# First mixer of a two-layer encoder: items in pairs, float32r masks, and value products placed behind the transposes of the weights

## The chip, the cores and the metric

The kernel runs on one core of one Trainium2 chip. The metric is the device time of one execution in microseconds (us). The core's engines are called as the profile calls them: PE is the matrix engine (PEld its weight loads), DVE the vector engine, ACT the scalar engine with the activation functions, POOL the general engine, SP the one that issues most transfers.

## The reference

A trunk of two layers is applied to two sequences, a prompt of 256 rows and a sample of 512 rows, 1024 wide, all in float32. Each layer runs a token mixer and then a SwiGLU block, each between two RMS norms, with a residual sum. The mixer of layer 0, the one that the change touches, is a windowed attention: 16 query heads of 64 in 4 groups, each group with one key and one value head, and a learned logit per head (a sink) in the denominator. A query row sees the keys at a distance of at most 128.

```
sc = einsum('bqkgd,bskd->bkgqs', qi, kb)
valid = (abs(qpos - kpos) <= WINDOW) & (kpos >= 0) & (kpos < s)
sc = where(valid, sc, -inf)
m = maximum(max(sc), sink)
e = exp(sc - m)
p = e / (sum(e) + exp(sink - m))
o = einsum('bkgqs,bskd->bqkgd', p, vb)
```

The mixer of layer 1 is a differential attention without a window; the change leaves it alone.

## The kernel before

The 768 rows are six tiles of 128 (tiles 0 and 1 the prompt, 2 to 5 the sample). Weight products run in float32r, with each operand split into a high and a low part, so that each 128-deep step of a product is three matrix products (L315, L316, L317). ACT makes the high part, DVE the low part.

The first mixer (`mixer_a`) goes through 24 units: for each of the 4 key heads, the six row tiles. `unit(i)` projects 384 columns (four query heads, one key and one value head) in eight steps and one end step, which applies the rotary positions and splits. Two units later a `turn` transposes the split queries and keys on PE (L609, L611) and ACT copies them out.

Attention follows its unit by `LAG` = 4 units. It is cut into 96 items (unit i, query head j of the four). `score` makes the scores of one item: queries times the high part of the keys (L630), times their low part (L631), and then, where a neighbouring key tile is only half inside the window, a product of an identity with a mask (L633 for the left, L635 for the right neighbour), which adds -3e38 to what must not be seen. Identity and masks are bf16 and 128 columns wide. Units with two key tiles (row tiles 0, 1, 2, 5) have one mask, those with three (row tiles 3, 4) have two. DVE takes the maximum (L637) and its negative with the sink (L640), ACT the exponential with its sum (L646) and that of the sink (L648). `normalize` makes the denominator on DVE (L655, L656) and scales the weights (L657). `turn_e` transposes the weights on PE, one product of 128 columns in full fp32 for each key tile (L666), and ACT copies them to a buffer of the unit (L670), heads 0 and 2 in one half of it, heads 1 and 3 in the other. `values` multiplies them with the values in full fp32 (L680): for each key tile one product for heads 0 and 2 and one for heads 1 and 3, which take the two halves of 64 output rows; the profile counts two instructions for each.

The order is written out in the loop at L704. `item(n)` issues the score of item n, the normalization of n-1 and the transposes of n-3. For each unit the list `att` holds four such items and then the value products of the unit before; `weave` spreads these five entries evenly among the nine or ten steps of the projection. From unit 23 on a special order holds, in which the output projection takes the place of the projection. The framework that builds the program keeps each engine's list in the order of the source, except that it moves later work in front of an instruction whose operands, by its own reckoning, are not ready.

The weights `e` of two items share one of three 128x1024 buffers (tag `y` of the pool `scr`), which also hold the normalized input tiles at the start. All products write to eight PSUM banks.

Of the kernel before, what the change touches and what calls it, by code (L numbers as in the profile page):

```python
# [8 lines left out]

F32 = mybir.dt.float32  # L10
F32R = mybir.dt.float32r
BF16 = mybir.dt.bfloat16
AF = mybir.ActivationFunctionType
ALU = mybir.AluOpType
AX = mybir.AxisListType
# [2 lines left out]
P = 128  # L18
D = 1024
# [19 lines left out]
def seq_of(t):  # L39
    for first, n in SEQS:  # L40
        if first <= t < first + n:
            return first, n
    raise ValueError(t)
# [3 lines left out]
def trunk(  # L47
# [19 lines left out]
    nc = tc.nc  # L67
    const = ctx.enter_context(tc.tile_pool(name="const", bufs=1))
# [5 lines left out]
    scr = ctx.enter_context(tc.tile_pool(name="scr", bufs=3))  # L74
# [3 lines left out]
    def bank(name):  # L78
        return ps.tile([P, 512], F32, tag="ps", name=name)


    ident = const.tile([P, P], F32, name="ident")
    make_identity(nc, ident)
    ident_r = const.tile([P, P], F32R, name="ident_r")
    nc.vector.tensor_copy(out=ident_r, in_=ident)
    ident_b = const.tile([P, P], BF16, name="ident_b")
    nc.vector.tensor_copy(out=ident_b, in_=ident)

    masks = []
    for name, step, mult in (("mask_l", 1, -1), ("mask_r", -1, 1)):  # L90
        m = const.tile([P, P], BF16, name=name)
        nc.gpsimd.memset(m, 0.0)
        nc.gpsimd.affine_select(
            out=m, in_=m, compare_op=ALU.is_ge, fill=MASK, base=0,
            pattern=[[step, P]], channel_multiplier=mult,
        )
        masks.append(m)
    cos_sb = const.tile([P, 4, HD], F32, name="cos_sb")
    sin_sb = const.tile([P, 4, HD], F32, name="sin_sb")
    mhalf = const.tile([P, 8], F32, name="mhalf")  # L100
# [190 lines left out]
    def take(n):  # L291

        i = state["used"]
        state["used"] += n
        prepare(i + n)
        return [parts.pop(j) for j in range(i, i + n)]
# [74 lines left out]
    def new_y(name):  # L371
        return scr.tile([P, D], F32, tag="y", name=f"y_{name}")
# [165 lines left out]
    def column_blocks(taken, width):  # L538
        return [tuple(w[:, j * width:(j + 1) * width] for w in s) for s in taken for j in range(2)]

    def out_unit(t, wk, o, n2, gp, sq, name):

        pm = bank(name)
        steps = product_steps(pm, [(htile(t, k), wk[k]) for k in range(KT)])
        if t == NT - 1:
            steps = releasing(steps, 4)
        return steps + [lambda: project_end(t, pm, o, n2, gp, sq, name)]  # L550
# [16 lines left out]
    def mixer_a(gp, g_next, first_steps, o):  # L567
        with ExitStack() as st:
# [53 lines left out]
            def score(i, j):  # L622
                gi, t = divmod(i, NT)
                first, n = seq_of(t)
                k0, k1 = max(first, t - 1), min(first + n, t + 2)
                nk = k1 - k0
                keys = slice((k0 - first) * P, (k1 - first) * P)
                s = bank(f"sc{i}_{j}")[:, :nk * P]
                left, right = k0 < t, k1 > t + 1
                nc.tensor.matmul(s, q[i][:, j], kh[gi, first][:, keys], start=True, stop=False)  # L630
                nc.tensor.matmul(s, q[i][:, j], kl[gi, first][:, keys], start=False, stop=not (left or right))  # L631
                if left:
                    nc.tensor.matmul(s[:, :P], ident_b, masks[0], start=False, stop=not right)  # L633
                if right:
                    nc.tensor.matmul(s[:, (nk - 1) * P:], ident_b, masks[1], start=False, stop=True)  # L635
                mx = small.tile([P, 1], F32, tag="mx", name=f"mx{i}_{j}")
                nc.vector.tensor_reduce(out=mx, in_=s, axis=AX.X, op=ALU.max)  # L637
                h = gi * 4 + j
                negm = small.tile([P, 1], F32, tag="negm", name=f"negm{i}_{j}")
                nc.vector.tensor_scalar(  # L640
                    out=negm, in0=mx, scalar1=-HD ** -0.5, scalar2=nsink[:, h:h + 1], op0=ALU.mult, op1=ALU.min)
                if j % 2 == 0:
                    e2[0] = new_y(f"e{i}_{j}")
                e = e2[0][:, j % 2 * 512:j % 2 * 512 + nk * P]
                den = small.tile([P, 2], F32, tag="den", name=f"den{i}_{j}")
                nc.scalar.activation(  # L646
                    out=e, in_=s, func=AF.Exp, bias=negm, scale=HD ** -0.5, accum_out=den[:, 0:1])
                nc.scalar.activation(out=den[:, 1:2], in_=negm, func=AF.Exp, bias=sink[:, h:h + 1])  # L648
                blocks[i, j] = e, den
# [3 lines left out]
            def normalize(i, j):  # L653
                e, den = blocks[i, j]
                nc.vector.tensor_tensor(out=den[:, 0:1], in0=den[:, 0:1], in1=den[:, 1:2], op=ALU.add)  # L655
                nc.vector.reciprocal(out=den[:, 0:1], in_=den[:, 0:1])  # L656
                nc.vector.tensor_scalar(out=e, in0=e, scalar1=den[:, 0:1], scalar2=None, op0=ALU.mult)  # L657
# [3 lines left out]
            def turn_e(i, j):  # L661
                e, _ = blocks.pop((i, j))
                nk = e.shape[1] // P
                tp = bank(f"tpe{i}_{j}")
                for c in range(nk):
                    nc.tensor.transpose(tp[:, c * P:(c + 1) * P], e[:, c * P:(c + 1) * P], ident)  # L666
                if j == 0:

                    eTs[i] = ap.tile([P, 3, 2, 2, P], F32, tag="eT", name=f"eT{i}", bufs=2)
                nc.scalar.copy(  # L670
                    out=eTs[i][:, :nk, j % 2, j // 2], in_=tp[:, :nk * P].rearrange("p (c n) -> p c n", c=nk))

            def values(i):
                gi, t = divmod(i, NT)
                first, n = seq_of(t)
                k0, k1 = max(first, t - 1), min(first + n, t + 2)
                po, eT = bank(f"poa{i}"), eTs.pop(i)
                for c in range(k1 - k0):
                    for r in range(2):
                        nc.tensor.matmul(  # L680
                            po[r * HD:(r + 1) * HD, :256], vv[gi, first][:, k0 + c - first],
                            eT[:, c, r].rearrange("p h n -> p (h n)"), start=(c == 0), stop=(c == k1 - k0 - 1))
                nc.scalar.copy(out=o[t][:, gi * 256:(gi + 1) * 256], in_=po[:, :256])

            def split_o(t):
                half, at = t // 3, (t % 3) * P
                split(h_hi[half][:, :, at:at + P], h_lo[half][:, :, at:at + P],
                      o[t].rearrange("p (k n) -> p k n", k=KT))

            LAG = 4  # L690
            n_units = 4 * NT
            items = [(i, j) for i in range(n_units) for j in range(4)]
            n_items = len(items)

            def item(n):
                if n < n_items:
                    score(*items[n])
                if 1 <= n <= n_items:
                    normalize(*items[n - 1])
                if 3 <= n <= n_items + 2:  # L700
                    turn_e(*items[n - 3])

            wk_o, sq = [], {}
            for i in range(n_units + LAG):  # L704
                if i < n_units:
                    fill = unit(i)
                    at = 4 if i == 0 else 3
                    fill = fill[:at] + first_steps.pop(i, []) + fill[at:]
                else:
                    t = i - n_units  # L710
                    if t == 0:
                        wk_o = column_blocks(take(4), 512)
                    fill = out_unit(t, wk_o, o, 0, gp, sq, f"po0_0_{t}")
                if i - 2 in pending:
                    fill = fill[:4] + [pending.pop(i - 2)] + fill[4:]
                att = []
                if i >= LAG:
                    for j in range(4):
                        n = (i - LAG) * 4 + j
                        att.append(lambda n=n: item(n))  # L720
                    if i > LAG:
                        att.append(lambda i=i: values(i - LAG - 1))
                if i >= n_units - 1:

                    t = i - n_units + 1
                    fill = (att[:1] + fill[:2] + att[1:2] + fill[2:3] + att[2:3] + fill[3:4] + att[4:] + fill[4:5]
                            + [lambda t=t: split_o(t)] + att[3:4] + fill[5:])
                    att = []
                weave(att, fill)

            fill = out_unit(LAG, wk_o, o, 0, gp, sq, f"po0_0_{LAG}")
            att = [lambda n=n: item(n) for n in range(n_items, n_items + 4)] + [lambda: values(n_units - 1)]
# [746 lines left out]
```

## Time and profile before

| | |
|---|---|
| time, median of 3 runs (lowest to highest) | 1687.2 us (1686.35 to 1689.65) |
| the profiled execution | 1688.34 us |
| its span from first to last instruction | 1686.6 us |
| mean granted clock of PE | 0.997 |
| PE busy in the span | 98% |
| DVE busy in the span | 74% |
| ACT busy in the span | 56% |

The profiled execution is one run with the profiler on; all times of instructions are read from it, in us from the start of its span. A group such as `sc<-mask_l,ident_b` names what is written, what streams through PE and what is loaded as weights. The length of a matrix product in the profile contains its way through the array and overlaps with the next one, so that what a product costs in a row of products is the distance to the start of the next.

### The profile page before, as it was taken

The page shows a single profiled execution, that of the slowest core. Times are in us where ns is not written, and L with a number is a line of the kernel's source. Part 1 is how long each engine was busy: PE and PEld are TensorE (multiplying, and loading weights), DVE is VectorE, ACT ScalarE, POOL GpSimd, SP SyncE. Part 2 cuts the span into 40 slices and gives each one's busy share as a digit, 9 for nine tenths or more (in the row PEclk, how much of TensorE's full clock was granted, in tenths as well). Part 3 has the DMA queues.
Part 4 walks back from the last instruction along what each step waited for, and adds up shares of the span by engine and source line. Part 5 has one row for each costly group of instructions (what it writes and reads, how often), then busy time and mean ns, then how long its engine had stood idle before and what let it go on. Part 6 is the DMA issues. An engine that isn't in the chain of part 4 may idle for free. (4 is left out here: it accounts for less than half of the span.)

```text
span 1686.6 us, 25513 instructions
## 1 busy us (share of the span) xinstructions
PE 1659.1 (98%) x9483; PEld 1514.3 (90%) x9483; DVE 1251.3 (74%) x2488; ACT 949.7 (56%) x2158; POOL 81.7 (5%) x104
## 2 busy tenths in 40 slices
PE   7999999999999999999999999999899999999998
PEld 7888878899999998888999999988799999998887
DVE  7888766896766666988777676874997666666886
ACT  6777775654444444556566666674744444444553
POOL 1000001000000000001000000331000000000001
PEclk9999999999999999999999999999999999999999
DMA  6111014534333347666211111113444343336765
GB/s 212 39 38 48 14 38 150 175 134 140 109 125 99 128 139 250 230 235 205 83 39 38 38 38 38 48 51 113 170 138 141 108 141 108 128 114 226 249 222 176
DMA packets 62107, 207.30 MB, mean 123 GB/s; under 512 B 6752, under 2 KB 8928, under 8 KB 61728
## 3 DMA queue, kind: packets, MB, share of 16 engines
q1 hardware_dynamic: 55152, 175.15, 30.8%
q0 software_dynamic: 6688, 30.28, 5.6%
q8 instruction: 74, 1.21, 0.3%
q14 instruction: 49, 0.40, 0.1%
q10 hardware_dynamic: 144, 0.26, 0.0%
HBM read 162.80 MB, written 42.86 MB: 122 GB/s over the span
## 5 line engine op out<-in xcount | busy, mean ns | idle before, releaser
L223 DVE TENSOR_TENSOR wlo<-wraw,whi 128x1024 fp32r<-128x1024 f32 (+2 forms) x180 | 204.9, 1144 | 173.9 <-ACT whi L222 172.7
L222 ACT CAST whi<-wraw 128x1024 fp32r<-128x1024 f32 (+2 forms) x180 | 176.5, 986 | 117.4 <-PE py L316 58.9
L315 PE MATMUL py<-hhi,whi 128*128 128x384 f32 x464 | 155.4, 335 | 0.8 <-ACT u L976 0.8
L317 PE MATMUL py<-hhi,wlo 128*128 128x384 f32 x464 | 155.0, 334 | 0.0
L316 PE MATMUL py<-hlo,whi 128*128 128x384 f32 x464 | 155.0, 334 | 0.0
L315 PE MATMUL pqb<-whi,hhi 128*128 128x384 f32 x384 | 136.5, 356 | 0.0
L316 PE MATMUL pqb<-wlo,hhi 128*128 128x384 f32 x384 | 128.9, 336 | 0.0
L317 PE MATMUL pqb<-whi,hlo 128*128 128x384 f32 x384 | 128.8, 335 | 0.0
L303 ACT CAST hhi<-araw 128x768 fp32r<-128x768 f32 (+1 forms) x74 | 57.6, 783 | 94.6 <-DMA araw<-act 94.2
L317 PE MATMUL pv<-whi,hlo 128*128 128x512 f32 (+1 forms) x240 | 92.2, 384 | 0.4 <-DVE hlo L304 0.4
L315 PE MATMUL pv<-whi,hhi 128*128 128x512 f32 (+1 forms) x240 | 92.4, 385 | 0.0
L316 PE MATMUL pv<-wlo,hhi 128*128 128x512 f32 (+1 forms) x240 | 92.1, 384 | 0.0
L304 DVE TENSOR_TENSOR hlo<-araw,hhi 128x768 fp32r<-128x768 f32 (+1 forms) x74 | 65.2, 889 | 32.3 <-ACT hhi L303 32.1
L315 PEld LDWEIGHTS py<-hhi,whi 128*128 128x128 f32 x464 | 87.1, 188 | 1.7 <-ACT u L976 1.4
L316 PEld LDWEIGHTS py<-hlo,whi 128*128 128x128 f32 x464 | 87.1, 188 | 0.0
L317 PEld LDWEIGHTS py<-hhi,wlo 128*128 128x128 f32 x464 | 87.1, 188 | 0.0
L315 PE MATMUL po<-whi,hhi 128*128 128x512 f32 x192 | 77.9, 406 | 0.2 <-ACT hhi L303 0.2
L317 PE MATMUL po<-whi,hlo 128*128 128x512 f32 x192 | 75.4, 393 | 0.2 <-DVE hlo L304 0.2
L316 PE MATMUL po<-wlo,hhi 128*128 128x512 f32 x192 | 75.3, 392 | 0.0
L315 PEld LDWEIGHTS pqb<-whi,hhi 128*128 128x128 f32 x384 | 72.3, 188 | 2.0 <-issue 1.7
L315 PE MATMUL pqa<-whi,hhi 128*128 128x384 f32 x192 | 73.9, 385 | 0.0
L315 PE MATMUL px<-hhi,whi 128*128 128x384 f32 x208 | 70.8, 342 | 2.7 <-ACT hhi L303 2.7
(303 smaller groups left out, 4829.6 us busy)
## 6 DMA issues: line engine op xcount, KB each, us to landing
act<-st POOLq DMA_DIRECT2D x22, 1344.0 KB, 6.6
wraw<-in_wgu SPq DMA_DIRECT2D x56, 512.0 KB, 4.6
araw<-act SPq DMA_DIRECT2D x70, 384.0 KB, 4.0
y_wraw<-in_wgu SPq DMA_DIRECT2D x40, 512.0 KB, 3.6
wraw<-in_wd SPq DMA_DIRECT2D x40, 512.0 KB, 3.9
wraw<-in_wb SPq DMA_DIRECT2D x32, 384.0 KB, 3.2
xd<-x SPq DMA_DIRECT2D x18, 512.0 KB, 3.0
x<-xd SPq DMA_DIRECT2D x18, 512.0 KB, 4.1
```

The costliest lines, as they stand in the source:

```text
L222: state["raw_hi"] = nc.scalar.copy(out=hi, in_=src)
L223: state["raw_lo"] = nc.vector.tensor_tensor(out=lo, in0=src, in1=hi.bitcast(F32), op=ALU.subtract)
L303: state["hi"] = nc.scalar.copy(out=hi, in_=src)
L304: state["lo"] = nc.vector.tensor_tensor(out=lo, in0=src, in1=hi.bitcast(F32), op=ALU.subtract)
L315: nc.tensor.matmul(out, ah, bh, start=start and i == 0, stop=False, skip_group_check=more)
L316: nc.tensor.matmul(out, ah, bl, start=False, stop=False, skip_group_check=more)
L317: nc.tensor.matmul(out, al, bh, start=False, stop=stop and i == last, skip_group_check=more)
```

## The change

Three things are changed. The identity for the masks and the masks themselves become float32r: the masks are built as f32 by POOL in a scratch tile and cast by DVE. `item` can issue two scores one after the other; then it normalizes all items before n and transposes all up to n-3. Units 4 to 22 of the loop (attention of units 0 to 18) use it with two items at a time, so that `att` has two entries instead of four; the rest goes one by one as before. And in these units the value products are no entry of their own but are issued right behind the second pair, whose transposes are the last two heads of the same unit.

```
-    ident_b = const.tile([P, P], BF16, name="ident_b")
-    nc.vector.tensor_copy(out=ident_b, in_=ident)
     masks = []
+    row = scr.tile([P, D], F32, tag="y", name="mask_rows")
     for name, step, mult in (("mask_l", 1, -1), ("mask_r", -1, 1)):
-        m = const.tile([P, P], BF16, name=name)
+        m = row[:, len(masks) * P:(len(masks) + 1) * P]
         nc.gpsimd.memset(m, 0.0)
         nc.gpsimd.affine_select(
             out=m, in_=m, compare_op=ALU.is_ge, fill=MASK, base=0,
             pattern=[[step, P]], channel_multiplier=mult,
         )
-        masks.append(m)
+        masks.append(const.tile([P, P], F32R, name=name))
+        nc.vector.tensor_copy(out=masks[-1], in_=m)
...
-                    nc.tensor.matmul(s[:, :P], ident_b, masks[0], start=False, stop=not right)
+                    nc.tensor.matmul(s[:, :P], ident_r, masks[0], start=False, stop=not right)
...
-                    nc.tensor.matmul(s[:, (nk - 1) * P:], ident_b, masks[1], start=False, stop=True)
+                    nc.tensor.matmul(s[:, (nk - 1) * P:], ident_r, masks[1], start=False, stop=True)
...
-            def item(n):
-                if n < n_items:
-                    score(*items[n])
-                if 1 <= n <= n_items:
-                    normalize(*items[n - 1])
-                if 3 <= n <= n_items + 2:
-                    turn_e(*items[n - 3])
+            done = {"normed": 0, "turned": 0}
+
+            def item(n, several=1):
+
+                for m in range(n, min(n + several, n_items)):
+                    score(*items[m])
+                while done["normed"] < min(n, n_items):
+                    normalize(*items[done["normed"]])
+                    done["normed"] += 1
+                while done["turned"] < min(n - 2, n_items):
+                    turn_e(*items[done["turned"]])
+                    done["turned"] += 1
...
                 if i >= LAG:
-                    for j in range(4):
+
+                    step = 2 if i < n_units - 1 else 1
+                    for j in range(0, 4, step):
                         n = (i - LAG) * 4 + j
-                        att.append(lambda n=n: item(n))
+                        att.append(lambda n=n, step=step: item(n, step))
                     if i > LAG:
-                        att.append(lambda i=i: values(i - LAG - 1))
+                        value = lambda i=i: values(i - LAG - 1)
+                        if step == 1:
+                            att.append(value)
+                        else:
+                            att[-1:] = [lambda a=att[-1], value=value: (a(), value())]
```

More of the change, by code (lines that the diff above doesn't have):

```diff
@@ L11 @@
 F32R = mybir.dt.float32r
-BF16 = mybir.dt.bfloat16
 AF = mybir.ActivationFunctionType
```

## The prediction

> **What bounds the kernel now.** I read the page first, then the busy time of the first mixer's stretch, then the matrix engine's timeline inside it. The page's first line:
>
> ```profile
> span 1686.6 us, 25513 instructions
> ```
>
> The change touches only the first mixer's attention and the constants ahead of it. Its stretch, in the view of busy time by window (window, length, then PE, PEld, DVE, ACT, POOL):
>
> ```profile
> 34.00:256.00 222.00, 221.56 (x1513) 185.43 (x1512) 174.19 (x636) 166.41 (x573) 0.00 (x0) 1.00 0.12 37
> ```
>
> PE is busy 221.56 of 222.00 us and the clock is full; DVE with 174.19 and ACT with 166.41 have room, which covers two scores' reductions and exponentials arriving at once (if it doesn't, the last rival holds). So what counts is how long PE takes for its own list, and whether the new order makes it wait. A busy PE says nothing about gaps between products (ends are modelled), so I take distances from one start to the next. The timeline of PE (start, length, line, operation, count):
>
> ```profile
> 151.67 0.23 PE L633 MATMUL sc<-mask_l,ident_b 128*128 128x128 bf16 x1
> 151.71 0.42 PE L315 MATMUL pqa<-whi,hhi 128*128 128x384 f32 x1
> 152.00 0.41 PE L666 MATMUL tpe<-ident,y_e 128*128 128x128 f32 x2
> 152.17 0.42 PE L316 MATMUL pqa<-wlo,hhi 128*128 128x384 f32 x1
> 152.43 0.34 PE L317 MATMUL pqa<-whi,hlo 128*128 128x384 f32 x1
> ...
> 152.95 0.34 PE L317 MATMUL pqa<-whi,hlo 128*128 128x384 f32 x1
> 153.22 1.08 PE L680 MATMUL poa<-eT,va 128*64 128x256 f32 x8
> 154.24 0.44 PE L315 MATMUL pqa<-whi,hhi 128*128 128x384 f32 x1
> 154.52 0.34 PE L316 MATMUL pqa<-wlo,hhi 128*128 128x384 f32 x1
> ...
> 155.10 0.23 PE L635 MATMUL sc<-mask_r,ident_b 128*128 128x128 bf16 x1
> 155.17 0.39 PE L666 MATMUL tpe<-ident,y_e 128*128 128x128 f32 x2
> 155.32 0.42 PE L315 MATMUL pqa<-whi,hhi 128*128 128x384 f32 x1
> 155.58 0.33 PE L316 MATMUL pqa<-wlo,hhi 128*128 128x384 f32 x1
> 155.75 0.34 PE L317 MATMUL pqa<-whi,hlo 128*128 128x384 f32 x1
> ```
>
> Three things are to be seen. A projection product of 384 columns takes 0.17 (155.58 to 155.75). A bf16 mask followed by transposes takes 0.07 (155.10 to 155.17). And the order on the chip is not the source's: at 151.71 one projection product stands between a mask and the transposes that the source puts directly behind it, so work that is not yet ready is passed by later work that is.
>
> **The change part by part.** Of the 24 units (4 key heads by 6 row tiles), 0 to 18 go in pairs: 76 items, 38 pairs. Units with two key tiles have one mask per item (13 units, 26 pairs), units with three have two (6 units, 12 pairs). Units 19 to 23 keep single items: 12 with one mask, 8 with two. The value products directly behind transposes are those of units 0 to 17, 18 calls. Instruction counts of DVE and ACT stay, except in the constants.
>
> First, transposes in one group instead of two. Two transposes and the projection product behind them run from 155.17 to 155.58; less that product's 0.17 they cost 0.24. For three key tiles:
>
> ```profile
> 174.20 0.23 PE L633 MATMUL sc<-mask_l,ident_b 128*128 128x128 bf16 x1
> 174.27 0.22 PE L635 MATMUL sc<-mask_r,ident_b 128*128 128x128 bf16 x1
> 174.32 0.50 PE L666 MATMUL tpe<-ident,y_e 128*128 128x128 f32 x3
> 174.57 0.43 PE L315 MATMUL pqa<-whi,hhi 128*128 128x384 f32 x1
> ```
>
> Three stand 0.25 ahead of the next product against 0.15 for two: 0.10 to 0.11 for each further one. A group of four is then 0.24 + 0.21 = 0.45 against 2 x 0.24 = 0.48, a gain of 0.03 a pair: 38 x 0.03 = -1.1 us. Switching from transposes to products costs very little here, which is the first reason why I expect no large gain.
>
> Second, the masks in float32r. The weight loads of PE:
>
> ```profile
> 155.10 0.10 PEld L635 LDWEIGHTS <-ident_b 128*128 128x128 bf16 x1
> 155.12 0.21 PEld L666 LDWEIGHTS tpe<-ident,y_e 128*128 128x128 f32 x2
> 155.29 0.19 PEld L315 LDWEIGHTS pqa<-whi,hhi 128*128 128x128 f32 x1
> 155.40 0.19 PEld L316 LDWEIGHTS pqa<-wlo,hhi 128*128 128x128 f32 x1
> ```
>
> The load of a float32r operand lasts 0.19, that of the bf16 identity 0.10. Where no long product covers them, two float32r loads start 0.11 apart (155.29, 155.40). A float32r mask streams only 128 columns, so the load for what follows is not covered: I take 0.11 where another mask or a score follows. Where transposes follow, I keep 0.07: their loads are the same as before. Bounds for a mask: 0.05, what the second bf16 mask takes (174.27 to 174.32), and 0.25, half the time per 256 columns of the full fp32 value products (four products, two beside each other, in 1.02). I take 0.11 because operand type, load and shape are nearest. A pair with one mask each: 0.11 + 0.07 against 0.14, +0.04, 26 times, +1.0. A pair with two each: 3 x 0.11 + 0.07 = 0.40 against 2 x 0.12, +0.16, 12 times, +1.9. Single items with two masks: 0.18 against 0.12, 8 times, +0.5. Sum +3.4 us.
>
> The Trainium skill, TensorE: Matmul & The Clock Gate, section Weight-path perf modes, speaks against this edit: fast weight load is on for 128 weights of a type that is not FP32, so the identity loses it; the trace agrees (0.10 against 0.19). Its section Back-to-back issue gap gives 81 ns for a sustained stream of loads and products of 128 columns; by that the masks would come to about +1.4 us, an estimate from that page, instead of +3.4.
>
> Third, the constants:
>
> ```profile
> 1.45 0.45 DVE L85 CAST ident_r<-ident 128x128 fp32r<-128x128 f32 x1 [0.52 <-POOL ident masks.py:199]
> 1.67 0.30 DVE L87 CAST ident_b<-ident 128x128 bf16<-128x128 f32 x1
> 6.76 1.28 DVE L369 SCALAR_TENSOR_TENSOR y_pre<-x,rstd_pre,gpre 128x1024 f32<-128x1024 f32 x1 [4.79 <-POOL mask_r L93]
> ```
>
> One DVE cast goes, two come, and POOL's two masks are written as f32. The cast of the second mask may be queued ahead of the first tile's scaling at 6.76, behind which PE's first work waits. Bounds 0 and 0.45 (the cast's row); I take +0.3. The scratch rows hold one of three big buffers until then, which only the third tile wants.
>
> Fourth, the value products. Entering them from a projection product costs 0.10 (152.95 to 153.22, less 0.17), the block 1.02 (to 154.24), the product behind it 0.11 more than usual (154.24 to 154.52): 1.23. Behind transposes the entry is not seen cleanly; I leave its 0.10, with 0 as the other bound. The Trainium skill, TensorEngine Tiling (Array Packing), section Key Properties, says that changing the tiling mode drains the engine; by it the entry stays also behind transposes, as these use 128 columns and the products 64.
>
> But the products of even heads (j = 0, 2) read ACT's copy for j = 2, those of odd heads the copy for j = 3, and both now come from the transposes directly in front. As work that is not ready is passed, projection products will go in between, and where the two copies fall apart in time, the call breaks in two. Unit 0 shows the price:
>
> ```profile
> 48.16 0.34 PE L317 MATMUL pqa<-whi,hlo 128*128 128x384 f32 x1
> 48.43 0.65 PE L680 MATMUL poa<-eT,va 128*64 128x256 f32 x2
> 49.01 0.45 PE L315 MATMUL pqa<-whi,hhi 128*128 128x384 f32 x1
> 49.29 0.34 PE L316 MATMUL pqa<-wlo,hhi 128*128 128x384 f32 x1
> 49.55 1.08 PE L680 MATMUL poa<-eT,va 128*64 128x256 f32 x6
> 50.56 0.44 PE L317 MATMUL pqa<-whi,hlo 128*128 128x384 f32 x1
> 50.84 0.28 PE L630 MATMUL sc<-kha,qa 128*128 128x256 f32 x1
> ```
>
> Two of eight products went ahead alone: 0.10 + 0.58 + 0.11, then 0.09 + 1.01 + 0.11, together 2.00 against 1.23. A break costs 0.77. What drives the copies apart is seen on ACT in another unit:
>
> ```profile
> 202.49 0.36 ACT L670 COPY eT<-tpe 128x256 f32<-128x256 f32 x1
> 202.74 0.48 ACT L646 ACTIVATE y_e<-sc,negm 128x256 f32<-128x256 f32 x1
> ...
> 203.39 0.37 ACT L670 COPY eT<-tpe 128x256 f32<-128x256 f32 x1
> ```
>
> An exponential between two copies makes 0.90 of what would be 0.25 (ACT starts its next instruction that much after a copy), longer than the lone product's 0.58. After the change both copies are issued behind two exponentials, in source order; an exponential that becomes ready between them goes first. I take 5 of 18 calls broken: +3.9 us; bounds 0 and 18, that is 0 and +13.9.
>
> Sum: -1.1 + 3.4 + 0.3 + 3.9 = +6.5 us. The profiled execution took 1688.34 us (span 1686.6 and 1.7 around it), 1.1 above the median 1687.2; on the median the sum gives 1693.7. A measurement of this kernel tells about 0.2% from no change, 3.4 us: below 1683.8 is faster, above 1690.6 slower.
>
> **The rivals.** *No break.* The copies follow each other at 0.25, or the value products slide behind projection products until both are there; then the change does not do what it says (they are not directly behind the transposes), and the sum is +2.6: 1689.8. For it: all but 3 of the old 24 calls came whole, by my count. Against: there the source had put other work between, here nothing.
>
> *The joins are free (faster).* If float32r loads hide behind scores, masks cost 0.05 to 0.07 throughout and the second term is 0; if value products join the fp32 transposes without their entry, 18 x 0.10 = -1.8; and if transposes, now normalized half a unit ahead, are never displaced, some 12 displacements by my count go at 0.11 each (151.67 to 152.43 less two products is 0.42, against 0.07 + 0.24): -1.3. With -1.1 and +0.3 that is -3.9: 1683.3. It decides from the point at which a mask followed by a score takes no more than 0.07. Against it: the loads 0.11 apart.
>
> *Full fp32 rate.* If 128 columns of float32r run like fp32, each of 128 masks takes 0.25 instead of 0.07 or 0.06: +23.7, with -1.1 and +0.3 near 1710. Against it: the 384-column products of this type run at 0.17.
>
> *The products hold PE.* If the value products are queued directly behind the transposes and wait there, everything on PE queues behind them; at 0.90 between copies 18 calls lose 16, with +2.6 near 1706. Against it: displaced work like that at 151.71.
>
> **How the numbers follow.** Broken calls 0.43 (time 1693.7, own range 1691 to 1704), no break 0.27, free joins 0.17, full fp32 rate 0.06, products that hold PE 0.07. The likeliest case gives 1693.7. The range 1683 to 1704 goes from free joins to all 18 calls broken; left out are the last two rivals, 0.13, and what lies below free joins. Faster 0.17; same 0.27, the case without a break; slower 0.43 + 0.06 + 0.07 = 0.56.
>
> **What would show it.** In the changed profile: masks as 128x128 float32r with loads of 0.19, 0.11 from a mask to the next score and 0.07 to a transpose; four or six transposes in one run with 0.10 to 0.11 each; runs of value products of x2 and x6 (or x10) with projection products between, in about 5 of units 0 to 17; the first scaling on DVE at about 7.1 instead of 6.76. Masks at 0.05 or 0.25, no broken runs, or PE idle ahead of value products would show the step wrong that they belong to. A shift of over 2 us outside the window from 34 to 256 would say that the cause lies elsewhere.

## The result, and the profile after

The changed kernel takes 1705.57 us (median of 4, 1704.41 to 1705.68) against 1686.97 (median of 4, 1686.35 to 1689.65): 18.6 us more, a ratio of 1.0101 with an interval of 1.0086 to 1.0116. The forecast was 1693.7, range 1683 to 1704. The direction was right; the loss is nearly three times the forecast one, and the time lies outside the range. The profiled execution took 1705.49 us. Its page, first line:

```profile
span 1703.7 us, 25491 instructions
```

That is 17.1 more than before's 1686.6. The stretch from 34 to 256 us in the view of busy time by window (PE, PEld, DVE, ACT, POOL, clock, DMA):

```profile
34.00:256.00 222.00, 217.24 (x1423) 186.62 (x1422) 170.31 (x609) 156.36 (x545) 0.00 (x0) 1.00 0.12 37
```

Two things changed against the same row of before: PE is no longer busy throughout (217.24 instead of 221.56), and it gets through fewer instructions in the same time (1423 instead of 1513), at the same full clock. So PE waits, and what it does takes longer. What it waits for stands in the view of waits, PE alone, 34 to 280 us (engine, line, releaser: us in total, times, longest):

```profile
PE poa L679 <- ACT eT L669: 4.4, 11, 1.0
PE tpe L665 <- DVE den L654: 0.2, 1, 0.2
```

Before, the same view had two waits of 0.2 for other operands and none of value products:

```profile
PE po L317 <- DVE hlo L304: 0.2, 1, 0.2
PE po L315 <- ACT hhi L303: 0.2, 1, 0.2
```

The groups by line and shape say where the work itself became longer (busy us, mean ns | idle time ahead). Before:

```profile
L680 PE MATMUL poa<-eT,va 128*64 128x256 f32 x224 | 31.4, 391 | 0.0
```

After (the second row is a weight load of a mask, needed further down):

```profile
L679 PE MATMUL poa<-eT,va 128*64 128x256 f32 x224 | 39.2, 392 | 4.5 <-ACT eT L669 4.4
L634 PEld LDWEIGHTS sc<-mask_r,ident_r 128*128 128x128 f32 x64 | 12.0, 188 | 0.0
```

The same 224 instructions of the value products, each as long as before (391 and 392 ns), cover 39.2 us instead of 31.4: fewer of them run beside each other. That is the sign to look for, since the mean alone shows nothing. The timeline of the changed kernel (rows of PE and ACT, `...` where some of them are left out) shows both ways in which it happens, and a wait:

```profile
143.26 0.83 PE L665 MATMUL tpe<-ident,y_e 128*128 128x128 f32 x6
143.81 0.48 ACT L669 COPY eT<-tpe 128x384 f32<-128x384 f32 x1 [0.22 <-PE tpe L665]
143.85 0.42 PE L314 MATMUL pqa<-whi,hhi 128*128 128x384 f32 x1
144.12 0.33 PE L315 MATMUL pqa<-wlo,hhi 128*128 128x384 f32 x1
144.38 0.65 PE L679 MATMUL poa<-eT,va 128*64 128x256 f32 x2
144.38 0.47 ACT L645 ACTIVATE y_e<-sc,negm 128x256 f32<-128x256 f32 x1
...
144.95 0.44 PE L316 MATMUL pqa<-whi,hlo 128*128 128x384 f32 x1
145.03 0.46 ACT L645 ACTIVATE y_e<-sc,negm 128x256 f32<-128x256 f32 x1
...
145.67 0.47 ACT L669 COPY eT<-tpe 128x384 f32<-128x384 f32 x1
...
146.37 1.51 PE L679 MATMUL poa<-eT,va 128*64 128x256 f32 x10
...
153.26 0.68 ACT L669 COPY eT<-tpe 128x256 f32<-128x256 f32 x2
153.46 0.33 PE L315 MATMUL pqa<-wlo,hhi 128*128 128x384 f32 x1
153.72 1.35 PE L679 MATMUL poa<-eT,va 128*64 128x256 f32 x8
...
155.00 0.44 PE L316 MATMUL pqa<-whi,hlo 128*128 128x384 f32 x1
...
162.07 0.33 PE L316 MATMUL pqa<-whi,hlo 128*128 128x384 f32 x1
162.33 0.67 ACT L669 COPY eT<-tpe 128x256 f32<-128x256 f32 x2
162.78 1.35 PE L679 MATMUL poa<-eT,va 128*64 128x256 f32 x8 [0.38 <-ACT eT L669]
```

At 143.81 ACT copies the transposes of one head, then does two exponentials, and copies the next head's only at 145.67. The first product of the even heads, whose copy is done, goes at 144.38, alone, for 0.57 (to 144.95); the rest of the call follows at 146.37. At 153.26 the two copies follow each other; the call stays whole, but takes 1.28 (153.72 to 155.00) instead of 1.01, because the first product of the odd heads starts at 153.99, just behind the end of the second copy (153.26 + 0.68), while that of the even heads started at 153.72. Ahead of 162.78 PE stands still for 0.38 until the first copy is done, although its list goes on with projection products behind the call. In none of the units 0 to 17 do value products start directly behind transposes: two to twelve projection products stand between (in before mostly five or six).

The table sums all of PE's time in the first mixer by what PE runs, from the start of the first score to the start of the last value product; that last product's 0.3 is in its own column only. Each entry is a distance from the start of a run of one kind to the start of the next run, so that waits count with the run ahead of them. Value calls are 24 in each kernel. "Broken" are those in two pieces, "late" those that are whole but 0.1 or more too long, because they begin out of step (for example 1.28 instead of 1.01 for two key tiles, 1.75 instead of 1.45 for three) or wait inside. Each row is one profiled execution.

| kernel | mixer us | scores | masks | projection, both transposes | value products | broken, late |
|---|---|---|---|---|---|---|
| before | 218.3 | 27.7 | 7.8 | 153.6 | 29.5 | 3, 0 |
| after | 234.6 | 29.9 | 9.5 | 158.8 | 36.8 | 11, 10 |
| `values_entry` | 228.3 | 29.0 | 9.6 | 154.9 | 35.2 | 1, 12 |
| `values_only` | 231.5 | 28.6 | 8.8 | 154.7 | 39.8 | 21, 0 |
| `masks_only` | 222.1 | 27.0 | 10.0 | 156.3 | 29.0 | 1, 2 |
| `pairs_bf16` | 226.9 | 32.0 | 7.1 | 154.7 | 33.5 | 4, 12 |
| `values_r10` | 226.8 | 29.9 | 9.7 | 159.7 | 27.8 | 0, 0 |
| `turn_first_r10` | 225.8 | 33.4 | 13.5 | 151.4 | 27.8 | 0, 0 |
| `values_next_pair` | 219.4 | 29.7 | 9.3 | 151.7 | 29.0 | 1, 2 |
| `before_r10` | 216.8 | 27.7 | 7.8 | 153.8 | 27.8 | 0, 0 |
| `next_single_r10` | 215.9 | 28.2 | 8.4 | 151.8 | 27.8 | 0, 0 |
| `values_next_pair_r10` | 219.0 | 29.7 | 9.3 | 152.5 | 27.8 | 0, 0 |
| `next_pair_r10_bf16` | 217.0 | 31.4 | 7.1 | 151.0 | 27.8 | 0, 0 |

Of the 17.1 us between the two spans, 16.3 lie in the mixer, 0.1 ahead of it, 0.7 behind it; the profiled executions of all these kernels differ by 1.9 ahead of the mixer and by over 5 behind it, where their programs are nearly the same, so that these two say nothing of the change. In the mixer: value products +7.3, scores and masks +3.9, the rest +5.2, in which the waits of 4.4 are contained.

### The profile page after: what moved, and what is told of

The parts are those of the page before. It is cut to its first block, busy times and chain, and to the rows that moved or that the text cites. A ratio compares the mean times of both kernels' runs of the same rounds, so it can differ in the third digit from the quotient of the medians.

```text
span 1703.7 us, 25491 instructions
## 1 busy us (share of the span) xinstructions
PE 1669.5 (98%) x9483; PEld 1525.7 (90%) x9483; DVE 1255.6 (74%) x2489; ACT 948.7 (56%) x2158; POOL 82.5 (5%) x104
## 5 line engine op out<-in xcount | busy, mean ns | idle before, releaser
L315 PEld LDWEIGHTS pqb<-wlo,hhi 128*128 128x128 f32 x384 | 72.4, 188 | 0.6 <-DVE wlo L222 0.5
```

The lines of the kernel that those rows point to most:

```text
L315: nc.tensor.matmul(out, ah, bl, start=False, stop=False, skip_group_check=more)
```

## The experiments

My theory when I began: PE's list is fixed when the program is built and is worked off in order; the changed list holds value products two to twelve projection products behind the transposes, while ACT, with two exponentials at once in its own list, delivers the copies later and farther apart. The rivals: the pairs themselves or the float32r masks cost the time, and the place of the value products doesn't matter. Each ratio below is taken against runs of the kernel before from the same session, whose medians went from 1688.1 to 1689.1, so that ratios compare better across sessions than times do.

### The value products an entry of their own again (`values_entry`)

```
-                        if step == 1:
-                            att.append(value)
-                        else:
-                            att[-1:] = [lambda a=att[-1], value=value: (a(), value())]
+                        att.append(value)
```

> The changed kernel, but the value products are an entry of their own again, spread with the two pairs among the projection steps. Theory (the place of the value products costs most: they break in two, start out of step or wait for ACT's copies): most of the 18.6 us goes; only the exposed loads of the float32r masks (+3.9) less the merged transposes (-1) stay, 1688 to 1691 us. Rival (the pairs themselves load DVE and ACT in bursts and make PE wait): 1700 or more.

Measured: 1697.05 us, ratio 1.0056 [1.0040, 1.0073]. It lies between the two. Not quite half of the loss (a ratio of 1.0056 instead of 1.0101) goes with the place of the value products; the rest stays, and it is not all masks: value products take 5.7 more than before, scores and masks 3.0. The view of waits:

```profile
PE poa L679 <- ACT eT L669: 2.6, 6, 0.6
PE tpe L665 <- DVE negm L639: 0.8, 1, 0.8
```

Only one call is broken, but 12 are late. In one of them, for example, the transposes start at 129.77 on PE, and ACT makes the two copies at 131.61 and 132.73, each behind an exponential (130.86 and 131.97); the call starts at 132.14 and waits inside until 133.26. So pairs make the copies late by themselves. The rival had that cause, but priced it too high; the theory had left it out.

### The value products alone (`values_only`)

The kernel before, with single items and bf16 masks; the value products go directly behind the last transposes of their unit.

```
-                        att.append(lambda i=i: values(i - LAG - 1))
+                        value = lambda i=i: values(i - LAG - 1)
+                        if i >= n_units - 1:
+                            att.append(value)
+                        else:
+                            att[2] = lambda a=att[2], value=value: (a(), value())
```

> The kernel before with one edit: the value products of a unit are issued right behind the item whose transposes are that unit's last, single items and bf16 masks kept. Theory: the products of heads 0 and 2 are ready about 1.6 us before those of heads 1 and 3 and go ahead alone, so 12 to 18 of the calls break at 0.77 us each: 1696 to 1701 us. Rival (only pairs make the copies fall apart): within 2 us of before.

Measured: 1700.6 us, ratio 1.0074 [1.0059, 1.0089], as the theory had it. Here PE doesn't wait for a copy at all; 21 of the 24 calls split instead, most of them like this one (timeline of PE):

```profile
150.54 0.39 PE L666 MATMUL tpe<-ident,y_e 128*128 128x128 f32 x2
150.86 0.65 PE L680 MATMUL poa<-eT,va 128*64 128x256 f32 x2
151.44 0.44 PE L315 MATMUL pqa<-whi,hhi 128*128 128x384 f32 x1
...
152.33 1.08 PE L680 MATMUL poa<-eT,va 128*64 128x256 f32 x6
153.34 0.44 PE L316 MATMUL pqa<-wlo,hhi 128*128 128x384 f32 x1
```

The even heads' first product, whose copies are old, stands directly behind the transposes, the rest four projection products later. 18 more broken calls cost 10.3 in the value products (29.5 to 39.8, 0.57 each) and 13.2 in the mixer as a whole, 0.73 each. The prediction's price of 0.77 for a break, taken from one call of unit 0, about holds; the number of breaks is what it had wrong.

### The masks alone, and everything without them (`masks_only`, `pairs_bf16`)

`masks_only` is the kernel before with the identity and the masks in float32r; `pairs_bf16` the changed kernel with both in bf16, as before.

```
-        m = const.tile([P, P], BF16, name=name)
+        m = row[:, len(masks) * P:(len(masks) + 1) * P]
...
-        masks.append(m)
+        masks.append(const.tile([P, P], F32R, name=name))
+        nc.vector.tensor_copy(out=masks[-1], in_=m)
```

> The kernel before with float32r masks and identity and nothing else. Theory (a float32r mask costs 0.11 where another score or mask follows, 0.06 to 0.07 where transposes follow): 32 items with two masks lose 0.05 each, +1.6, some displaced transposes gain: 1686.5 to 1689.5 us. Rival (the masks carry a large part of the loss): 1692 or more.

Measured: 1692.16 us, ratio 1.0019 [1.0007, 1.0030]. In us that is the rival's bound, but the kernel before took 1688.91 in the same session; the difference of 3.2 lies between the two expectations. In the table the masks take 2.2 more and the scores 0.7 less, so that the type's own cost is near the expected 1.6. In its profiled run three waits of transposes for DVE (2.2 us in total) come on top; whether they belong to every execution stays open.

> The changed kernel with the masks and their identity in bf16 again. Theory: a bf16 mask ahead of a score exposes the same float32r load and more (0.15 by 158.31 to 158.45 in the trace of before, against 0.11 measured for float32r), but a second mask behind a mask costs 0.06 instead of 0.11; about even, 13 to 20 us above before. Rival (the float32r masks are a main part of the loss): 10 us or less above before.

Measured: 1697.5 us, ratio 1.0049 [1.0033, 1.0064]: the rival's number, but not for the rival's reason. With bf16 masks, scores and masks together take 39.1 us, with float32r 39.4: in pairs the type makes next to no difference to these two. What a pair costs is seen in the timeline of PE in `pairs_bf16`:

```profile
142.92 0.28 PE L630 MATMUL sc<-kha,qa 128*128 128x256 f32 x1
143.04 0.28 PE L631 MATMUL sc<-kla,qa 128*128 128x256 f32 x1
143.16 0.23 PE L635 MATMUL sc<-mask_r,ident_b 128*128 128x128 bf16 x1
143.19 0.36 PE L630 MATMUL sc<-kha,qa 128*128 128x256 f32 x1
143.40 0.28 PE L631 MATMUL sc<-kla,qa 128*128 128x256 f32 x1
143.52 0.23 PE L635 MATMUL sc<-mask_r,ident_b 128*128 128x128 bf16 x1
143.59 0.61 PE L666 MATMUL tpe<-ident,y_e 128*128 128x128 f32 x4
```

and in the changed kernel:

```profile
152.30 0.28 PE L630 MATMUL sc<-kla,qa 128*128 128x256 f32 x1
152.41 0.22 PE L634 MATMUL sc<-mask_r,ident_r 128*128 128x128 f32 x1
152.47 0.33 PE L629 MATMUL sc<-kha,qa 128*128 128x256 f32 x1
152.65 0.28 PE L630 MATMUL sc<-kla,qa 128*128 128x256 f32 x1
152.77 0.22 PE L634 MATMUL sc<-mask_r,ident_r 128*128 128x128 f32 x1
152.82 0.62 PE L665 MATMUL tpe<-ident,y_e 128*128 128x128 f32 x4
153.20 0.42 PE L314 MATMUL pqa<-whi,hhi 128*128 128x384 f32 x1
```

The first score product behind a projection product takes 0.12 (142.92 to 143.04). Behind a mask it takes 0.21 with bf16 (143.19 to 143.40) and 0.18 with float32r (152.47 to 152.65), and the mask ahead of it 0.03 and 0.06: 0.24 together by either. So a short mask does not cover what the score needs, whatever the mask's type. The 7.7 us by which its mixer is below the changed one's lie elsewhere: 3.3 in the value products, with 4 broken calls instead of 11, and 4.1 in projection and transposes, 0.9 of it in waits (3.5 instead of 4.4), in a list that came out differently. Why a mask's type moves value products in the list isn't settled.

### Heads 1 and 3 first (`values_r10`, `before_r10`)

The same one line in the changed kernel and in the one before. The copy of head 3 comes last; a call that begins with heads 1 and 3 can't start until all its operands are there.

```
-                    for r in range(2):
+                    for r in (1, 0):
```

> The changed kernel with the two halves of the value products exchanged: heads 1 and 3 first, so that the first product waits for the later of the two copies. Theory: no call breaks or starts out of step any more (10 x 0.77 and 8 x 0.27 = 9.9 us less), PE's waits for the copies stay at 4 to 6 us: 1694 to 1697 us. Rival (the waits are what costs, and holding back the first product makes them longer): 1703 or more.

Measured: 1698.04 us, ratio 1.0056 [1.0041, 1.0071], 1 us above the theory's range and 5 below the rival's. No call is broken or late, and the value products take 27.8 instead of 36.8. The groups and the waits:

```profile
L679 PE MATMUL poa<-eT,va 128*64 128x256 f32 x224 | 29.5, 390 | 6.3 <-ACT eT L669 6.2
```

```profile
PE poa L679 <- ACT eT L669: 6.2, 17, 1.5
```

One line that only makes each call wait for its last copy removes every broken and every late call: they are one thing, a copy that isn't there when the call begins. And beginning early earned nothing: waiting for the last copy costs 1.8 more in waits and saves 9.0 in the value products.

> The kernel before with one edit: in the value products heads 1 and 3 come first. Theory (a call breaks when the first product is ready ahead of the rest; before has 3 broken calls): no broken call is left, 3 x 0.77 = 2.3 us less in the first mixer, 1 to 2.5 us below before. Rival (in those places PE would have had to wait anyway): within 0.5 us of before.

Measured: 1687.24 us, ratio 0.9982 [0.9973, 0.9991], as the theory had it. The kernel before had three broken calls of its own (units 0, 18 and 19); without them the value products take 1.7 less, 0.57 for each, and the mixer 1.6 less. The profiled run was the slowest of the eleven.

### Transposes ahead of scores (`turn_first_r10`)

The changed kernel with heads 1 and 3 first, and in each pair the transposes are issued ahead of the scores, so that ACT's copies stand ahead of the new exponentials in its list.

```
             def item(n, several=1):
+                while done["turned"] < min(n - 2, n_items):
+                    turn_e(*items[done["turned"]])
+                    done["turned"] += 1
                 for m in range(n, min(n + several, n_items)):
                     score(*items[m])
...
-                while done["turned"] < min(n - 2, n_items):
-                    turn_e(*items[done["turned"]])
-                    done["turned"] += 1
```

> The changed kernel with heads 1 and 3 first, and in each pair the transposes of the weights issued ahead of the two scores, so that ACT's copies stand ahead of the two exponentials. Theory (PE waits because the copies are queued behind exponentials): the 6.2 us of waits of the kernel with only the first of these edits fall under 2; 4 to 6 us above before. Rival (the value products come too soon after the transposes whatever ACT does in between): 8 or more above before.

Measured: 1696.16 us, ratio 1.0040 [1.0026, 1.0054], with waits of 4.3 instead of 6.2 in the same view. That is 7.1 above before, between the two, and decides little. The copies' place in ACT's list may be part of the wait, but two thirds of it stay. PE's list came out differently too: nine value calls now stand directly behind the masks of a pair, with 1.7 of waits ahead of them, which the table counts under masks. Against `values_r10`, scores and masks take 7.3 more, projection and transposes 8.3 less. What the place of the copies alone is worth can't be told from this run.

### The value products behind the next unit's first pair (`values_next_pair`)

The changed kernel, where the value products are directly behind transposes in the source, but behind those of the next unit, half a unit later.

```
-                    if i > LAG:
-                        value = lambda i=i: values(i - LAG - 1)
-                        if step == 1:
-                            att.append(value)
-                        else:
-                            att[-1:] = [lambda a=att[-1], value=value: (a(), value())]
+                    if i >= n_units - 1:
+                        att.append(lambda i=i: values(i - LAG - 1))
+                    u = i - LAG - 2
+                    if u >= 0 and i < n_units:
+                        att[0] = lambda a=att[0], u=u: (a(), values(u))
```

> The changed kernel with the value products of a unit behind the first pair of the next unit, that is directly behind transposes whose copies they do not need. Theory: no broken call and no wait for copies; what is left are the exposed loads of the masks, 2 to 5 us above before; if joining fp32 transposes saves the entry of 0.10, 2 us less than that. Rival (pairs in bursts make PE wait elsewhere): 7 or more above before.

Measured: 1689.4 us, ratio 1.0002 [0.9993, 1.0012]. All of the loss is gone with the pairs and the float32r masks still in. The timeline of PE now shows what the change set out to make, in all of units 0 to 17:

```profile
147.26 0.62 PE L665 MATMUL tpe<-ident,y_e 128*128 128x128 f32 x4
147.81 1.08 PE L679 MATMUL poa<-eT,va 128*64 128x256 f32 x8
148.82 0.45 PE L314 MATMUL pqa<-whi,hhi 128*128 128x384 f32 x1
```

The call is whole and takes 1.01, and no wait of a value product is left in the view of waits. Projection and transposes take 1.9 less than before (151.7 against 153.6), which gives back over half of the 3.5 that scores and masks take more (39.0 against 35.5).

### Towards a better version

Three combinations. `next_single_r10` is the kernel before with heads 1 and 3 first and the value products behind the next unit's first transposes (single items, bf16 masks). `values_next_pair_r10` is `values_next_pair` with that order of heads, and `next_pair_r10_bf16` the same with bf16 masks. The edits are those shown above.

> The kernel before with heads 1 and 3 first in the value products, and with the value products of units 0 to 17 issued directly behind the first transposes of the next unit, single items, bf16 masks. Theory: what hurt behind the last transposes was the copies that they had to wait for; here all four copies are done before, so no call breaks, none starts out of step, PE doesn't wait, and entering behind transposes costs no more than behind projection products: at or below the kernel before with heads 1 and 3 first, 0.995 to 0.998 of the kernel before (1679 to 1684 where that takes 1687). Rival: the position itself costs, by the entry into the tiling of the value products behind transposes (0.1 for each of 18 calls and more): 1.000 to 1.003.

Measured: 1684.9 us, ratio 0.9982 [0.9973, 0.9991]: as far below as `before_r10`, just short of the theory's 0.998, and the interval excludes the rival. All 18 calls stand behind transposes, whole; the mixer takes 2.4 less than before. What joining gives beyond the order of heads, 0.9 in the mixer, can't be told apart in the times.

> The changed kernel with the value products behind the first pair of the next unit and heads 1 and 3 first. Theory: the one or two broken or late calls left in the unpaired tail go, 1 to 2 us below the same kernel without the heads' order (1.0002), so 0.9985 to 0.9997 of the kernel before; float32r masks still cost their 3 or so. Rival: as pairs deliver their copies by twos, the heads' order changes nothing: 1.000 to 1.001.

Measured: 1689.25 us, ratio 1.0003 [0.9994, 1.0012]: the rival's number. The value products are all whole (27.8), but the mixer is only 0.4 shorter, less than these times can show.

> The same with bf16 masks: pairs are all that is left of the change. Theory: pairing saves about 2 (transposes in one group, fewer changes between transposes and products), the masks' 2 to 4 go, the broken calls too: 0.995 to 0.998 of the kernel before, below both kernels. Rival: pairs make DVE or ACT late, or the builder's order displaces as much as the joins save (as with bf16 masks in pairs before): 0.999 or more.

Measured: 1686.69 us, ratio 0.9992 [0.9983, 1.0001], the rival's number. Against `before_r10`, projection and transposes take 2.8 less, scores and masks 3.0 more: what pairs and joined value products save there, pairs lose at the second score.

These last two kernels differ in the type of the masks alone. Their medians are 2.6 us apart (1689.25 and 1686.69), their mixers 2.0: 0.5 in scores and masks, 1.5 in projection and transposes, which no run explains. By these two, float32r masks still cost 2 to 3 us in pairs, most of it outside the scores and masks themselves.

## Why the prediction was wrong in size

Each term against what was measured:

- **Transposes in one group, -1.1.** Four and the projection product behind them take 0.64 (152.82 to 153.46); less that product's 0.17 it is 0.47, where 0.45 was forecast. After taking the waits (4.4) and the changes to and from the eight extra pieces (8 x 0.2, the part of 0.77 that lies outside the products) out of the +5.2 of projection and transposes, -0.8 is left. Right.
- **Masks, +3.4.** Scores and masks took 3.9 more. A single mask ahead of a score took 0.06 and made the score product behind it 0.06 longer, together about the forecast 0.11; ahead of transposes it took 0.06. Of two masks in a row the first took 0.06 and the second 0.11 (starts at 132.89 and 132.95, the transposes at 133.06), where the forecast had it the other way round, with nearly the same sum. The size was right, its cause only half: by `pairs_bf16` the order alone makes most of it, since the bf16 mask of a pair doesn't cover the score behind it either. The rule of the Trainium skill that I had set against this edit (TensorE: Matmul & The Clock Gate, section Weight-path perf modes) is borne out by the load, 188 ns in the row of `ident_r`. In pairs it is not borne out by the time of scores and masks; what the type costs there besides is the unexplained 1.5 above.
- **Constants, +0.3.** The first scaling on DVE started at 7.05 instead of 6.76, as forecast. The first score came 0.1 later, which is less than the profiled executions differ at that place (33.8 to 35.6 us), so that no cost of it is shown.
- **Value products, +3.9.** This step failed. "I take 5 of 18 calls broken" should have been 10 of 18; the other 8 were not whole and undisturbed, as I had assumed, but began out of step, at 0.27 each; and the waits, which the sum held at nothing, were 4.4. Value products +7.3, extra changes 1.6 and waits 4.4 make 13.3 instead of 3.9: 9.4 of the 10.6 between the forecast +6.5 and the measured +17.1 of the profiled execution. The rest are masks (0.5) and 0.7 behind the mixer; the misses of the transposes (0.3) and of the constants (-0.2) about cancel.

Three assumptions led there. I read 151.71, where a projection product had slipped ahead, as a behaviour of the chip that would go on: work that isn't ready is passed. In the changed kernel PE stood still 11 times ahead of value products, 4.4 us in all, and at 162.78 with projection products right behind in its list. So nothing passed them there. What stands ahead of its place in the source must then have been put there when the framework ordered the list; this fits all the traces, but no run here looks into how it reckons. Next, I wrote that both copies are issued behind two exponentials, but priced only what comes between them, not that the first copy is late as well. And I took 1.23 as the price of any call that stays whole, although its own rows showed two halves of the array that must start together.

Of the rivals, *No break* and *The joins are free* are excluded by the time; *Full fp32 rate* by masks at 0.06 to 0.11. *The products hold PE* (1706) came nearest in time and has its share, 4.4 of the 17; but its condition, products directly behind the transposes, was met in none of units 0 to 17, and in `values_r10`, where no call is broken or late and PE waits 6.2, the total is 1698. Twice as much of the loss, 8.9, is work spread out rather than PE standing still.

The range reached to 1704, as if all 18 calls were broken and nothing else; waits belonged inside it, since broken calls, late calls and waits all come from copies that aren't there when the call begins: with the value products half a unit later (`values_next_pair`), all three are gone from units 0 to 17.

## What to carry to other kernels

When work is moved up to its producer, trace every operand back to the engine that makes it and ask what that engine will have queued ahead of it; an order written into the list doesn't adapt, and PE waits where an operand is later than its place in the list. For products that share the array in halves, let the half whose operand comes last go first, and look at the busy time of the group against its count: the same instructions covering more time means that they no longer run beside each other. Moving the consumer half a unit later removed the whole loss here, though it gave no gain over the kernel before.

## What the runs showed of the hardware

Two value products in the two halves of the array start 6 to 7 ns apart when both are ready, and three take as long as four (1.01 for six instructions at 152.33 and for eight at 147.81), so that a product left alone costs its whole 0.57. One that starts 0.27 ahead of its partner (153.72 and 153.99) makes the call 0.27 longer.

Entering the value products is dearer behind transposes than behind projection products. Four transposes and the way to what follows take 0.55 if that is a value product (147.26 to 147.81) and 0.38 if it is a projection product (152.82 to 153.20): the entry costs 0.17 there, where the prediction took 0.10, its figure behind projection products, and 0 as the other bound. The Trainium skill, TensorEngine Tiling (Array Packing), section Key Properties, says that a change of the tiling mode drains the engine; the trace agrees in that the entry is not free behind transposes, but shows no drain as such. Joining still gains a little in the mixer: `next_single_r10` takes 2.0 less than `before_r10` in projection and transposes and 1.1 more in scores and masks. In the times that gain isn't seen.
